# A two-layer hybrid decoder trunk: stacked keys and queries by transfers within SBUF, and latents and conv gates left unscaled ahead of their norms

## The chip, the cores and the metric

The kernel runs on one core of one Trainium2 chip. The metric is device time in microseconds for one execution of the whole program, the median over runs.

## The reference

Two layers over 1024 tokens with a model width of 1024, all in float32. Each layer normalises its input, projects it once, splits the result among four mixers, normalises each mixer's output, projects back, and then runs a gated feed-forward block of width 2816.

```python
def rmsnorm(x, g):
    y = x * lax.rsqrt(jnp.mean(x * x, axis=-1, keepdims=True) + 1e-6)
    return y * g

for l in range(2):
    proj = rmsnorm(x, attn_norm[l]) @ w_in[l]
    (c_q, c_kv, k_r, g_b, g_c, u_conv, u_pool, q_sw, k_sw, v_sw) = jnp.split(proj, pts, axis=-1)
    # 4 heads; q = rmsnorm(c_q) @ w_uq, k, v = rmsnorm(c_kv) @ w_ukv, one shared rotary key k_r
    y_a = mla_attention(c_q, c_kv, k_r, ...)
    y_b = g_b * causal_conv3(g_c * u_conv)
    y_c = multiscale_pool(u_pool, pool_w[l], pool_scale[l])
    # 4 query heads, 2 key heads of 64, window 128, sinks
    y_d = swa_sink_attention(q_sw, k_sw, v_sw, swa_sinks[l], slopes)
    mixed = concat(rms(y_a), rms(y_b), rms(y_c), rms(y_d)) * mix_norm[l]
    x = x + mixed @ w_o[l]
    gate, up = jnp.split(rmsnorm(x, ffn_norm[l]) @ w_gate_up[l], 2, axis=-1)
    x = x + (silu(gate) * up) @ w_down[l]
return rmsnorm(x, final_norm)
```

## The kernel before

Everything is held transposed: 128 channels on the partitions, tokens along the free axis, in two halves t of 512 tokens. A matrix product in float32 is made from three fast products: each operand is split into a high part (a cast to fp32r, by ScalarE, `act`) and a low part (the operand less the high part, by VectorE, `dve`). `split`, `half_split` (L278 to L291) do that, and `mm3` (L269) issues the three matmuls per 128 rows of contraction. A square tile of 128 channels by 512 tokens has a contraction over 8 such blocks, so 24 matmuls.

SBUF is handed out by `Slots` as 47 places of 128 x 1024 values, each a pair of halves; freed places go to the back of a queue. A tile that takes a place over waits until everything that used the place is done. PSUM has eight banks with the tags mm (2), s (3), t (2) and pv (1). All bulk loads and stores are issued by `sp` (SyncE), in the order of its queue; an issue whose wait isn't over holds up those behind it. Weights are fetched one step ahead by `expect`, `take` and `ahead`. The program is written as one sequence, and a scheduler decides, when the kernel is built, the order of the instructions on each engine, so that matmuls of the next projection stand between the short steps of attention. That order is then fixed.

A layer's first part goes so:

- `SumSq` adds up squares of the layer's input; its `rnorm` (L323) sums over the partitions by a matmul with ones (L327) and makes r, the reciprocal root mean square, with Ln, Exp, Square and one correction step (L329 to L335). The projections run on the input without r, and each result is multiplied by r (`mul_to`, L339) when it leaves PSUM.
- Window attention's keys (`kk`, L462 to L471): the projection has key head 0 in rows 0 to 63 (`hd`) and head 1 in rows 64 to 127 (`tl`). Each head is wanted in both halves of a tile, once as high parts, once as low parts. ScalarE copies 64 rows to their own place and to the other half (L468, L469), VectorE makes the low parts for both (L470, L471).
- Window queries (`swa_q`, L417 to L432): for two heads e and o, one tile holds the high part of a head in one half and its low part in the other, so that two matmuls (L502, in `swa_unit`) do for a score block what three would.
- `conv` (L626) makes (u r)(C r), a convolution over three tokens, and multiplies with (B r). The second half of its channels, `conv(1)`, runs later, between the first steps of latent attention.
- Latent queries `cq` and keys `ckv` (from L730) are scaled by r, split with the gain, squared and summed (`sq_q`, `sq_kv`), and their own norm factor is applied later: for queries in the rotary tables `tq`, for keys before the split.
- The rotary key goes by a matmul with a selection matrix (L778) to rows 64 to 127; both key sets `kb_[0]` and `kb_[1]` get it by a split each. `keys(hp)` (L835) projects two heads' keys at a time and splits rows 0 to 63 and 64 to 127 of the result into rows 0 to 63 of `kb_[0]` and `kb_[1]`.
- `scores` (L863; matmuls L887 to L889), `mix_values` (L933), `out_some` and the feed-forward part follow. The steps over (head, half) are in `steps`; `keys(1)` runs at the fifth of them.

Of the kernel before, what the change touches and what calls it, by code (L numbers as in the profile page):

```python
# [13 lines left out]
AF = mybir.ActivationFunctionType  # L14
# [3 lines left out]
P = 128  # L18
# [92 lines left out]
def trunk_kernel(ctx: ExitStack, tc: tile.TileContext, ins, out):  # L111
# [183 lines left out]
    class SumSq:  # L295


        def __init__(self, n):
            self.n = n
            self.acc = [None, None]  # L300
            self.done = {}

        def add(self, t, f, cols=whole):
# [11 lines left out]
            act.activation(q, f, AF.Square)  # L315
            if m == self.n // P:
                dve.scalar_tensor_tensor(
                    out=a, in0=q, scalar=e, in1=a, op0=ALU.add, op1=ALU.add
                )
            else:  # L320
                dve.tensor_tensor(out=a, in0=a, in1=q, op=ALU.add)

        def rnorm(self, t, cols=whole, tag="t"):  # L323

            a, n = F.ap(self.acc[t])[:, cols], self.n
            p = ps(tag)[:, cols]
            pe.matmul(p, ones, a, start=True, stop=True)  # L327
            r0, q = tmp("tn")[:, cols], tmp("tn")[:, cols]
            act.activation(r0, p, AF.Ln, scale=1.0 / n)  # L329
            act.activation(r0, r0, AF.Exp, scale=-0.5)  # L330
            act.activation(q, r0, AF.Square)
            dve.scalar_tensor_tensor(
                out=q, in0=p, scalar=-0.5 / n, in1=q, op0=ALU.mult, op1=ALU.mult
            )
# [8 lines left out]

    hd = slice(0, 64)
    tl = slice(64, 128)

    x_in = ins["xT"]
    ss = SumSq(D)
# [11 lines left out]
    def enter_norm(t):  # L360
        for k in range(NK):
            ss.add(t, F.ap(xf[k][t]))
            F.free(xf[k][t])
        ratt[t] = ss.rnorm(t)

    def finish(x, t, cols):

# [10 lines left out]
    for l in range(L):  # L378
# [38 lines left out]
        def swa_q(m, pp):  # L417
            for t in range(2):
                f = tmp()
                dve.scalar_tensor_tensor(  # L420
                    out=f, in0=pp[t], scalar=0.125, in1=r_of(t), op0=ALU.mult, op1=ALU.mult
                )
                e, o = R.half(), R.half()
                qs[2 * m][t], qs[2 * m + 1][t] = e, o
                act.copy(R.ap(e)[hd], f[hd])
                act.copy(R.ap(o)[tl], f[tl])
                dve.tensor_tensor(
                    out=R.ap(e)[tl], in0=f[hd], in1=rd(R.ap(e)[hd]), op=ALU.subtract
                )
                dve.tensor_tensor(  # L430
                    out=R.ap(o)[hd], in0=f[tl], in1=rd(R.ap(o)[tl]), op=ALU.subtract
                )  # L432

        wk = take()
        if l == 0:
# [24 lines left out]
        pq = [proj(w, 0, "s"), proj(w, 1, "t")]  # L460
        ahead()
        kk = [[R.pair(), R.pair()] for _ in range(2)]  # L462
        for t in range(2):
            f = tmp()
            mul_to(f, pk[t], r_of(t))
            for g, own, oth in ((0, hd, tl), (1, tl, hd)):
                k1, k2 = R.ap(kk[g][0] + t), R.ap(kk[g][1] + t)
                act.copy(k1[own], f[own])  # L468
                act.copy(k1[oth], f[own])  # L469
                dve.tensor_tensor(out=k2[own], in0=f[own], in1=rd(k1[own]), op=ALU.subtract)  # L470
# [130 lines left out]

        def group_scale(g):

            sg = SumSq(2 * P)
# [21 lines left out]
        def conv(ct):  # L626

            z = F.pair()
            pp = project()
            for t in range(2):  # L630
                mul_to(F.ap(z + t), pp[t], r_of(t))
            yield
            pp = project()
            for t in range(2):
                f = tmp()
                mul_to(f, pp[t], r_of(t))
                mul_to(F.ap(z + t), F.ap(z + t), f)
# [21 lines left out]
            yield  # L659

        for _ in conv(0):
            swa_some(3)
        swa_q(1, project())
# [66 lines left out]
        sq_q = SumSq(2 * P)  # L730
# [10 lines left out]
        sq_kv = SumSq(P)  # L741
# [15 lines left out]
        for t in range(2):  # L757
# [424 lines left out]
        pieces = (0, 3, 2, 2, 1, 1, 2, 2)  # L1182
        conv1 = conv(1)
        next(conv1)
        group_scale("d")
        keys(0)
        group_split("d", 1)
# [2 lines left out]
        for n, (h, t) in enumerate(steps):  # L1190
# [8 lines left out]
            if n == 0:  # L1199
                group_split("d", 0)  # L1200
                next(conv1)
                for k in range(NK):
                    for u in range(2):
                        for s in hh[k][u]:
                            R.free(s)
                for u in range(2):
                    F.free(ratt[u])
                qn = queries(*steps[1])
                values()
                group_scale("b")  # L1210
                group_split("b", 1)
                group_split("b", 0)
                fetch_x()
                fetch_x()
# [366 lines left out]
        for n, (c, m) in enumerate(units):  # L1581
# [41 lines left out]
            elif c == B22:  # L1623
                done(2 * m, 1)
                if m == 0:
                    expect_layer(l + 1)
                    ahead()
                if m == 1:
                    ratt[0] = ss.rnorm(0, tag="pv")
                if m == NM - 1:  # L1630
                    ratt[1] = ss.rnorm(1, tag="pv")
# [139 lines left out]
```

## Time and profile before

| | |
|---|---|
| median of 3 runs | 2094.0 us (2093.92 to 2096.62) |
| span of the profiled execution | 2092.6 us |
| TensorE busy (PE) | 2057.8 us, 98% |
| VectorE busy (DVE) | 1493.1 us, 71% |
| ScalarE busy (ACT) | 977.7 us, 47% |
| GpSimd busy (POOL) | 539.8 us, 26% |
| granted TensorE clock, mean | 0.998 |

The span runs from the first to the last instruction of one profiled execution; the runs' times are taken without the profiler, and the median lies 1.4 us above the span. "PEld" is TensorE's loading of weights, which overlaps the matmuls. In a group's row, the columns are line, engine, operation, output from inputs by the program's names, shapes, and the count; behind the first bar the busy time in us and the mean of one in ns; behind the second the idle time of the engine just before, and who ended it. In a row of waits stand the waiting engine, tile and line, the releaser, and then the sum in us, the number and the longest. A stretch's row has the stretch, its length, busy time and count for PE, PE's loads, DVE, ACT and POOL, the granted clock, the DMA engines' busy share and GB/s. A DMA row has the tile, the issuing queue, the count, the size and the median time in us from issue to landing. u stands for any tile of `Slots`, te, tn and tp for short-lived tiles, vraw for a small raw weight.

### The profile page before, as it was taken

What the parts mean: (1) busy time and instruction counts of PE and PEld (TensorE: products, weight loads), DVE (VectorE), ACT (ScalarE), POOL (GpSimd) and SP (SyncE); (2) the same over time, 40 slices, a digit from 0 to 9 for tenths busy, and PEclk for the clock granted to TensorE, in tenths of its full rate; (3) what the DMA queues carried; (4) which work ended last, traced back from release to release, by engine and by line L of the source; (5) the groups of instructions that cost most, each with busy time, mean ns of one, the idle gap of its engine ahead of it and who ended that gap; (6) DMA issues with size and microseconds to landing.
All of it is one profiled execution on the core that took longest, in us unless ns stands there. A gap on an engine that the chain in (4) does not pass through costs nothing.

```text
span 2092.6 us, 26301 instructions
## 1 busy us (share of the span) xinstructions
PE 2057.8 (98%) x9442; PEld 1679.2 (80%) x9442; DVE 1493.1 (71%) x2407; ACT 977.7 (47%) x1706; POOL 539.8 (26%) x453
## 2 busy tenths in 40 slices
PE   8999999999999999999999999999999999999997
PEld 6777787888888888888888777877878888888887
DVE  6878977877666767566656889869666676675655
ACT  6446656653333334454433566657423333344442
POOL 0000000037676674200000000000467667541000
PEclk9999999999999999999999999999999999999999
DMA  4010122424444446886401102232354444378752
GB/s 178 33 51 26 68 87 73 161 72 169 172 156 151 166 161 201 290 289 220 147 28 51 46 13 92 68 117 100 112 180 161 143 174 156 126 259 312 260 178 88
DMA packets 148819, 289.76 MB, mean 138 GB/s; under 512 B 12608, under 2 KB 72000, under 8 KB 148688
## 3 DMA queue, kind: packets, MB, share of 16 engines
q1 hardware_dynamic: 148656, 288.03, 39.8%
q8 instruction: 74, 1.21, 0.2%
q14 instruction: 57, 0.47, 0.1%
q0 software_dynamic: 32, 0.04, 0.0%
HBM read 204.66 MB, written 83.36 MB: 138 GB/s over the span
## 4 chain that ended last, share of the span: by engine, by line
PE 92%; DVE 4%; ACT 2%; DMA 1%; issue 1%; POOL 0%; DVEq 0%; ACTq 0%; SPq 0%; POOLq 0%
PE ps_mm L269 35%; PE ps_s L269 28%; PE ps_t L269 12%; PE ps_pv L269 8%; PE ps_pv L953 2%; PE ps_t L941 1%; PE ps_t L327 1%; PE ps_s L887 1%; PE ps_pv L563 1%; PE ps_s L888 1%; PE ps_t L551 1%; PE ps_s L889 1%; PE ps_s L502 0%; DMA u<-in_w_o 0%; DVE u L281 0%
## 5 line engine op out<-in xcount | busy, mean ns | idle before, releaser
L269 PE MATMUL ps_mm<-u,u 128*128 128x512 f32 (+1 forms) x3376 | 825.2, 391 | 10.6 <-ACT u L283 6.9
L269 PEld LDWEIGHTS ps_mm<-u,u 128*128 128x128 f32 x3376 | 616.8, 189 | 132.9 <-ACT u L283 6.9
L269 PE MATMUL ps_s<-u,u 128*128 128x512 f32 x2672 | 630.8, 390 | 3.5 <-ACT tn L1167 3.5
L269 PEld LDWEIGHTS ps_s<-u,u 128*128 128x128 f32 x2672 | 501.5, 188 | 110.4 <-ACT tn L1167 4.3
L281 DVE TENSOR_TENSOR u<-u,u 128x1024 fp32r<-128x1024 f32 (+2 forms) x368 | 423.6, 1167 | 175.5 <-ACT u L280 155.3
L280 ACT CAST u<-u 128x1024 fp32r<-128x1024 f32 (+2 forms) x368 | 321.4, 897 | 485.1 <-PE ps_mm L269 182.3
L269 PE MATMUL ps_t<-u,u 128*128 128x512 f32 (+1 forms) x1212 | 274.5, 379 | 0.0
L269 PEld LDWEIGHTS ps_t<-u,u 128*128 128x128 f32 x1212 | 219.1, 188 | 44.1 <-issue 1.4
L950 POOL MEMSET u<- 128x128 f32 x32 | 6.4, 225 | 870.5 <-PE ps_mm L269 653.5
L158 POOL TENSOR_TENSOR u<-u 128x256 f32<-128x256 f32 x176 | 187.0, 1063 | 92.6 <-DMA u<-in_w_dn 62.7
L1303 POOL TENSOR_TENSOR tp<-tp,u 128x512 f32<-128x512 f32 x88 | 127.0, 1444 | 291.2 <-ACT tp L1302 290.9
L269 PE MATMUL ps_pv<-u,u 128*128 128x512 f32 x696 | 164.9, 389 | 0.0
L269 PEld LDWEIGHTS ps_pv<-u,u 128*128 128x128 f32 x696 | 130.7, 188 | 27.1
L1302 ACT ACTIVATE tp<-tp 128x512 f32<-128x512 f32 x88 | 55.5, 632 | 123.0 <-DVE tp L339 122.1
L280 ACT CAST u<-ps_t 128x512 fp32r<-128x512 f32 (+4 forms) x136 | 66.3, 505 | 67.4 <-PE ps_t L941 42.8
L281 DVE TENSOR_TENSOR u<-ps_t,u 128x512 fp32r<-128x512 f32 (+4 forms) x136 | 77.5, 582 | 25.7 <-ACT u L280 24.8
L283 ACT ACTIVATE u<-u,par 128x512 fp32r<-128x512 f32 x100 | 69.4, 715 | 51.2 <-DVE u L1090 16.5
L1123 POOL TENSOR_TENSOR u<-u,u 128x512 f32<-128x512 f32 x38 | 65.6, 1727 | 85.5 <-PE ps_s L269 44.5
L284 DVE SCALAR_TENSOR_TENSOR u<-u,par,u 128x512 fp32r<-128x512 f32 x100 | 72.8, 745 | 9.4 <-ACT u L283 9.1
L1515 DVE TENSOR_TENSOR tp<-ps_mm,tn 128x512 f32<-128x512 f32 x38 | 26.3, 692 | 68.7 <-PE ps_mm L269 68.7
L213 DVE TENSOR_TENSOR u<-u,u 128x1024 fp32r<-128x1024 f32 (+1 forms) x46 | 51.7, 1128 | 29.0 <-PE ps_t L269 10.0
L1296 DVE SCALAR_TENSOR_TENSOR u<-te,tp 128x512 f32<-128x512 f32 x38 | 44.9, 1182 | 36.8 <-POOL tp L1303 36.8
(188 smaller groups left out, 2248.7 us busy)
## 6 DMA issues: line engine op xcount, KB each, us to landing
u<-in_w_gu SPq DMA_DIRECT2D x88, 512.0 KB, 4.0
ad<-u SPq DMA_DIRECT2D x154, 256.0 KB, 2.2
u<-ad SPq DMA_DIRECT2D x70, 512.0 KB, 5.4
u<-in_w_dn SPq DMA_DIRECT2D x68, 512.0 KB, 3.8
qd<-u SPq DMA_DIRECT2D x44, 512.0 KB, 2.9
u<-qd SPq DMA_DIRECT2D x32, 512.0 KB, 5.2
u<-in_w_in SPq DMA_DIRECT2D x30, 512.0 KB, 3.5
u<-in_xT SPq DMA_DIRECT2D x32, 256.0 KB, 4.5
```

Source lines behind the costliest of these rows:

```text
L158: pool.tensor_tensor(out=o, in0=o, in1=u, op=ALU.add)
L213: dve.tensor_tensor(out=lo[:, :n], in0=raw[:, :n], in1=rd(hi[:, :n]), op=ALU.subtract)
L269: pe.matmul(o, w, r, start=start and k == 0 and i == 0, stop=stop and k == n - 1 and i == 2, skip_group_check=again,)
L280: act.copy(hi, f)
L281: dve.tensor_tensor(out=lo, in0=f, in1=rd(hi), op=ALU.subtract)
L283: act.activation(hi, f, AF.Copy, scale=gain)
L284: dve.scalar_tensor_tensor(out=lo, in0=f, scalar=gain, in1=rd(hi), op0=ALU.mult, op1=ALU.subtract)
L953: pe.matmul(py[:, c0:], v_of(j, h), R.ap(s)[:, c0:], start=j == 0 and n == 0, stop=j == nj - 1 and n == 1,)
L1123: pool.tensor_tensor(out=F.ap(q + 1), in0=a21, in1=a22, op=ALU.add)
L1296: dve.scalar_tensor_tensor(out=o, in0=a, scalar=-1.0, in1=b, op0=ALU.mult, op1=ALU.mult)
L1302: last_silu = act.activation(g, g, AF.Silu)
L1303: pool.tensor_tensor(out=g, in0=g, in1=r, op=ALU.mult)
```

## The change

1. `move(o, a)` is an SBUF to SBUF transfer issued by SyncE. It takes the place of casts and subtractions that made the same values a second time in another half of the partitions: for the window keys (six transfers of 64 rows by 1024 columns a layer, two of them after the other four have read), the window queries (two for each of four tiles, the second after the first, for it writes what the first reads), the rotary key and the latent keys (two for each half of the tokens, and four for each half and head pair; 64 rows by 512).
2. Latent queries and keys are no longer multiplied by r. Their norm is taken of the raw projection, with eps divided by r squared: c r / sqrt(mean((c r)^2) + eps) = c / sqrt(mean(c^2) + eps / r^2). `rnorm` with `more` keeps eps / r^2 (as eps times the mean square of the input, from the same PSUM bank) and r^2, and `SumSq` with `eps` adds the first in. The query latents are read in PSUM by cast, subtraction and square.
3. In `conv`, u is multiplied by r^2, C is used as it is and so is B; group b's norm gets eps / r^2.
4. r is freed after the second product of `conv(1)`, the eps tiles after group b's norm.

```diff
@@ SumSq.add
             if m == 1:
                 act.activation(a, f, AF.Square)
-                if self.n == P:
+                if self.eps:
+                    dve.scalar_tensor_tensor(
+                        out=a, in0=F.ap(self.eps[t]), scalar=float(self.n // P),
+                        in1=a, op0=ALU.mult, op1=ALU.add,
+                    )
+                elif self.n == P:
                     dve.tensor_scalar(out=a, in0=a, scalar1=e, scalar2=None, op0=ALU.add)
                 return
...
-            if m == self.n // P:
+            if m == self.n // P and not self.eps:
@@ SumSq.rnorm
             act.activation(r0, p, AF.Ln, scale=1.0 / n)
             act.activation(r0, r0, AF.Exp, scale=-0.5)
+            if more:
+                self.more[t] = F.half(), F.half()
+                r2, e = (F.ap(i) for i in self.more[t])
+                act.activation(e, p, AF.Copy, scale=EPS / n)
...
+            if more:
+                act.activation(r2, a, AF.Square)
@@
+    def move(o, a):
+        sp.dma_start(rd(o), rd(a))
@@ swa_q
-                e, o = R.half(), R.half()
+                e, o, h = R.half(), R.half(), R.half()
                 qs[2 * m][t], qs[2 * m + 1][t] = e, o
+                split(R.ap(h), R.ap(o), f)
                 act.copy(R.ap(e)[hd], f[hd])
-                act.copy(R.ap(o)[tl], f[tl])
-                dve.tensor_tensor(
-                    out=R.ap(e)[tl], in0=f[hd], in1=rd(R.ap(e)[hd]), op=ALU.subtract
-                )
-                dve.tensor_tensor(
-                    out=R.ap(o)[hd], in0=f[tl], in1=rd(R.ap(o)[tl]), op=ALU.subtract
-                )
+                move(R.ap(e)[tl], R.ap(o)[hd])
+                move(R.ap(o)[hd], R.ap(h)[tl])
+                R.free(h)
@@ window keys
+        f = F.pair()
         for t in range(2):
-            f = tmp()
-            mul_to(f, pk[t], r_of(t))
-            for g, own, oth in ((0, hd, tl), (1, tl, hd)):
-                k1, k2 = R.ap(kk[g][0] + t), R.ap(kk[g][1] + t)
-                act.copy(k1[own], f[own])
-                act.copy(k1[oth], f[own])
-                dve.tensor_tensor(out=k2[own], in0=f[own], in1=rd(k1[own]), op=ALU.subtract)
-                dve.tensor_tensor(out=k2[oth], in0=f[own], in1=rd(k1[own]), op=ALU.subtract)
+            mul_to(F.ap(f + t), pk[t], r_of(t))
+        split(*(R.ap2(i) for i in kk[0]), F.ap2(f))
+        F.free_pair(f)
+        for a, b in zip(kk[0], kk[1]):
+            for rows in (hd, tl):
+                move(R.ap2(b)[rows], R.ap2(a)[tl])
+        for a in kk[0]:
+            move(R.ap2(a)[tl], R.ap2(a)[hd])
@@ conv
-                mul_to(F.ap(z + t), pp[t], r_of(t))
+                mul_to(F.ap(z + t), pp[t], F.ap(rr[t][0]))
...
-                f = tmp()
-                mul_to(f, pp[t], r_of(t))
-                mul_to(F.ap(z + t), F.ap(z + t), f)
+                mul_to(F.ap(z + t), pp[t], F.ap(z + t))
...
-                f = tmp()
-                mul_to(f, pp[t], r_of(t))
-                mul_to(F.ap(ac + t), F.ap(ac + t), f)
+                mul_to(F.ap(ac + t), pp[t], F.ap(ac + t))
@@ latent queries and keys
-                f = tmp()
-                mul_to(f, pp[t], r_of(t))
-                cq[m][t] = half_split(f, pcol(l, PC_QN + m))
-                sq_q.add(t, f)
+                cq[m][t] = half_split(pp[t], pcol(l, PC_QN + m))
+                sq_q.add(t, pp[t])
...
-            mul_to(F.ap(s), pp[t], r_of(t))
+            act.copy(F.ap(s), pp[t])
@@ rotary key
             for s in range(2):
                 kb_[s][0][t], kb_[s][1][t] = R.half(), R.half()
-                split(R.ap(kb_[s][0][t])[tl], R.ap(kb_[s][1][t])[tl], p[tl])
+            split(R.ap(kb_[0][0][t])[tl], R.ap(kb_[0][1][t])[tl], p[tl])
+            for n in range(2):
+                move(R.ap(kb_[1][n][t])[tl], R.ap(kb_[0][n][t])[tl])
@@ keys
-                for s, own in ((0, hd), (1, tl)):
-                    split(R.ap(kb_[s][0][t])[hd], R.ap(kb_[s][1][t])[hd], p[own])
+                hl = half_split(p)
+                for n in range(2):
+                    for s, own in ((0, hd), (1, tl)):
+                        move(R.ap(kb_[s][n][t])[hd], R.ap(hl[n])[own])
+                    R.free(hl[n])
```

More of the change, by code (lines that the diff above doesn't have):

```diff
@@ L295, in trunk_kernel, with __init__ @@
     class SumSq:
-        def __init__(self, n):
+        def __init__(self, n, eps=None):
             self.n = n
+            self.eps = eps
             self.acc = [None, None]
             self.done = {}
+            self.more = [None, None]
         def add(self, t, f, cols=whole):
@@ L310, in add @@
                 act.activation(a, f, AF.Square)
-                if self.n == P:
+                if self.eps:
+                    dve.scalar_tensor_tensor(
+                        out=a,
+                        in0=F.ap(self.eps[t]),
+                        scalar=float(self.n // P),
+                        in1=a,
+                        op0=ALU.mult,
+                        op1=ALU.add,
+                    )
+                elif self.n == P:
                     dve.tensor_scalar(out=a, in0=a, scalar1=e, scalar2=None, op0=ALU.add)
@@ L321, in add, with rnorm @@
                 dve.tensor_tensor(out=a, in0=a, in1=q, op=ALU.add)
-        def rnorm(self, t, cols=whole, tag="t"):
+        def rnorm(self, t, cols=whole, tag="t", more=False):
             a, n = F.ap(self.acc[t])[:, cols], self.n
@@ L363, in enter_norm @@
             F.free(xf[k][t])
-        ratt[t] = ss.rnorm(t)
+        ratt[t] = ss.rnorm(t, more=True)
     def finish(x, t, cols):
@@ L602, in group_scale @@
         def group_scale(g):
-            sg = SumSq(2 * P)
+            sg = SumSq(2 * P, rr_eps if g == "b" else None)
             for t in range(2):
@@ L654, in conv @@
             for t in range(2):
-                f = tmp()
-                mul_to(f, pp[t], r_of(t))
-                mul_to(F.ap(ac + t), F.ap(ac + t), f)
+                mul_to(F.ap(ac + t), pp[t], F.ap(ac + t))
             y["b"][ct] = [ac, ac + 1]
             yield
+        rr = ss.more
+        rr_eps = [e for _, e in rr]
         for _ in conv(0):
@@ L729, in trunk_kernel @@
         cq = [[None, None], [None, None]]
-        sq_q = SumSq(2 * P)
+        sq_q = SumSq(2 * P, rr_eps)
         for m in range(2):
@@ L740, in trunk_kernel @@
         ckv = [None, None]
-        sq_kv = SumSq(P)
+        sq_kv = SumSq(P, rr_eps)
         pp = project()
@@ L1184, in trunk_kernel @@
         next(conv1)
+        for u in range(2):
+            F.free(ratt[u])
+            F.free(rr[u][0])
         group_scale("d")
@@ L1205, in trunk_kernel @@
                             R.free(s)
-                for u in range(2):
-                    F.free(ratt[u])
                 qn = queries(*steps[1])
@@ L1210, in trunk_kernel @@
                 group_scale("b")
+                for i in rr_eps:
+                    F.free(i)
                 group_split("b", 1)
@@ L1628, in trunk_kernel @@
                 if m == 1:
-                    ratt[0] = ss.rnorm(0, tag="pv")
+                    ratt[0] = ss.rnorm(0, tag="pv", more=not last)
                 if m == NM - 1:
-                    ratt[1] = ss.rnorm(1, tag="pv")
+                    ratt[1] = ss.rnorm(1, tag="pv", more=not last)
         for cols in (slice(0, 256), slice(256, HT)) if last else ():
```

## The prediction

> **What bounds the kernel now.** I read the page's head first, then the chain in order of time, the stretches of the span, and last TensorE's own waits.
>
> ```profile
> span 2092.6 us, 26301 instructions
> PE 2057.8 (98%) x9442; PEld 1679.2 (80%) x9442; DVE 1493.1 (71%) x2407; ACT 977.7 (47%) x1706; POOL 539.8 (26%) x453
> L269 PE MATMUL ps_mm<-u,u 128*128 128x512 f32 (+1 forms) x3376 | 825.2, 391 | 10.6 <-ACT u L283 6.9
> ...
> 404.28 5.44 PE ps_mm L269 x24
> ```
>
> TensorE is the bound: the span is its matmuls end to end. 24 of them in a row take 5.44 us, 0.227 us each, though one record lasts 0.391: they overlap, so each idle stretch shown below costs about 0.16 us more than it shows. The change adds and removes no matmul, so it can only move the idle places. Where they lie (the mixers run in the first five stretches of layer 0 and in 1077 to 1440 of layer 1):
>
> ```profile
> 8.00:60.00 52.00, 49.74 (x211) 39.58 (x212) 41.63 (x65) 35.55 (x60) 0.00 (x0) 1.00 0.38 144
> 60.00:205.00 145.00, 144.06 (x687) 113.43 (x686) 117.14 (x284) 78.48 (x185) 0.00 (x0) 1.00 0.12 40
> 205.00:260.00 55.00, 53.04 (x249) 42.17 (x248) 53.23 (x115) 36.13 (x78) 0.34 (x2) 1.00 0.18 63
> 260.00:345.00 85.00, 84.61 (x438) 67.99 (x436) 69.73 (x194) 52.80 (x134) 2.05 (x10) 1.00 0.24 76
> 345.00:405.00 60.00, 58.29 (x264) 45.98 (x265) 45.87 (x73) 34.22 (x58) 0.76 (x4) 1.00 0.42 147
> 405.00:1077.00 672.00, 670.64 (x2950) 553.43 (x2949) 443.69 (x501) 275.66 (x376) 268.20 (x208) 1.00 0.51 175
> 1077.00:1235.00 158.00, 157.26 (x752) 124.35 (x750) 121.63 (x292) 80.90 (x190) 0.00 (x0) 1.00 0.11 37
> 1235.00:1290.00 55.00, 53.07 (x248) 42.19 (x247) 53.26 (x113) 36.36 (x80) 0.35 (x2) 1.00 0.18 58
> ```
>
> The columns are the stretch, its length, then busy time of PE, PE's loads, DVE, ACT, POOL. Length less PE is idle: 2.26, 0.94, 1.96, 0.39, 1.71 in layer 0; 0.74 and 1.93 in layer 1 to 1290. In 205 to 260 and its twin DVE is busy 53.23 of 55, so it is the late engine there; elsewhere it has room. The idle of the stretches that hold the edited projections (first three, and the two of layer 1) is 2.26+0.94+1.96+0.74+1.93 = 7.8 us: about all that can be won.
>
> ```profile
> PE ps_t L327 <- DVE u L317: 2.2, 4, 0.9
> PE ps_s L887 <- ACT u L280: 2.0, 2, 1.0
> PE ps_mm L269 <- ACT u L212: 1.7, 2, 1.1
> PE ps_mm L269 <- ACT tn L315: 0.9, 1, 0.9
> PE ps_s L502 <- DVE u L430: 0.5, 1, 0.5
> ...
> 231.27 0.69 DVE L339 TENSOR_TENSOR te<-ps_s,u 128x512 f32<-128x512 f32 x1
> 232.00 0.62 ACT L280 CAST u<-te 128x512 fp32r<-128x512 f32 x1
> 232.67 0.50 PE L887 MATMUL ps_s<-u,u 128*128 128x512 f32 x1 [1.04 <-ACT u L280]
> ```
>
> The largest in 205 to 260 is read as a chain: the first latent query is scaled by DVE at 231.27, cast by ACT at 232.00, and the first score matmul starts at 232.67 after 1.04 idle. DVE came to that scaling late, behind the second conv half's products.
>
> **The change part by part.** Prices:
>
> ```profile
> L339 DVE TENSOR_TENSOR te<-ps_mm,u 128x512 f32<-128x512 f32 x22 | 15.1, 684 | 1.3 <-PE ps_mm L269 1.1
> L281 DVE TENSOR_TENSOR u<-ps_s,u 64x512 fp32r<-64x512 f32 x8 | 5.5, 685 | 0.8 <-ACT u L280 0.6
> L213 DVE TENSOR_TENSOR u<-u,u 128x1024 fp32r<-128x1024 f32 x15 | 18.1, 1219 | 5.4 <-PE ps_mm L269 4.4 <-PE ps_pv L563 1.0
> L332 DVE SCALAR_TENSOR_TENSOR tn<-ps_t,tn 128x512 f32<-128x512 f32 x14 | 9.6, 688 | 9.8 <-ACT tn L331 9.6
> L483 DVE TENSOR_TENSOR u<-ps_t,u 128x256 fp32r<-128x256 f32 x4 | 1.7, 418 | 0.3 <-ACT u L482 0.3
> L283 ACT ACTIVATE u<-u,par 128x512 fp32r<-128x512 f32 x45 | 30.8, 713 | 11.4 <-DVE u L339 5.1 <-DVE u L1090 5.1 <-DMA par<-in_params 0.7
> L212 ACT CAST u<-u 128x1024 fp32r<-128x1024 f32 x15 | 15.7, 1049 | 13.2 <-DMA u<-in_w_in 12.2 <-DVE u L580 0.7 <-DVE tn L332 0.3
> L330 ACT ACTIVATE tn<-tn 128x512 f32<-128x512 f32 x14 | 8.9, 633 | 0.3
> L280 ACT CAST u<-ps_s 64x512 fp32r<-64x512 f32 x8 | 4.7, 582 | 3.0 <-PE ps_s L269 2.9
> L482 ACT CAST u<-ps_t 128x256 fp32r<-128x256 f32 x4 | 1.5, 364 | 1.1 <-DVE u L483 1.1
> L941 PE MATMUL ps_t<-cst,u 128*128 128x128 f32 x144 | 23.3, 273 | 0.7 <-DVE u L281 0.7
> ...
> vraw<-in_w_uq SPq DMA_DIRECT2D x16, 128.0 KB, 2.1
> ad<-u SPq DMA_DIRECT2D x154, 256.0 KB, 2.2
> vraw<-in_pool_w SPq DMA_DIRECT2D x2, 128.0 KB, 5.1
> u<-ad SPq DMA_DIRECT2D x14, 256.0 KB, 5.9
> ...
> L209 SPq DMA_DIRECT2D vraw<-in_w_uq x16: 327/328/770, 27.6 to 1312.7; - x16
> ...
> L470 DVE TENSOR_TENSOR u<-te,u x8: 677/687/689, 40.4 to 1065.4; 64x512 fp32r<-64x512 f32 x8
> L427 DVE TENSOR_TENSOR u<-te,u x8: 684/685/686, 57.0 to 1138.1; 64x512 fp32r<-64x512 f32 x8
> ```
>
> A 64-row operation costs what a 128-row one does (0.685 against 0.684), so copying halves by engine is dear. Per layer DVE loses: window keys, eight subtractions for one of 1024 columns (8x0.687-1.219 = 4.3 us); one subtraction for each of four query tiles (2.7); two for the rotary key, four for the latent keys (4.1); four conv products (2.7, and as many for the second conv half, 2.7); four query-latent scalings, two key-latent ones which go to ACT (4.1). It gains two multiply-adds for the query latents and two for conv's group norm (2.8). Net about 18 us a layer. ACT loses some 7 us (seven casts of the window keys, six of 64 rows) and gains some 4 (four eps copies and squares of r, two copies of the key latent, 0.6 each). Nearly all of this lies under matmuls and is worth nothing by itself; with the cover gone it would be its length.
>
> *Gain in 205 to 260.* In the 26 us ahead of 231.27 fall four conv products and two key subtractions fewer and one or two multiply-adds more: 6x0.685-2x0.688 = 2.7 us of a DVE that never rests there. The query's scaling needs to come 1.04+0.16 earlier: all of that stall goes. The other stall (L327 behind L317, 0.9) is the group norm of the conv channels, whose chain gets one operation of 0.69 longer while its queue gets 2.7 shorter: I take half, 0.45. Bounds 0 and 1.96; taken 1.5 a layer, 3.0 in all.
>
> *Gain in 8 to 60.* DVE is rid of eight subtractions, ACT of seven casts, around the norm chain. Waits there that these feed: 0.9 and 0.5, with 0.16 each on top. Bounds 0 and 1.7; taken 0.8, since the two new ACT operations (1.2) stand in the norm's own queue.
>
> *Cost: the window keys wait for two transfers in a row.* In the changed order the first window score stands behind 74 matmuls of 512 columns and 8 transposes after the second norm's sum (50 and 8 before): 74x0.227+8x0.11 = 17.7 us of cover (a transpose is a record of 0.273 less the same 0.16). The chain, by rows: four ACT operations (0.6, 0.6, 0.63, 0.63) and a weight cast 1.05 = 3.5; three on DVE = 5.6; the 1024 cast and subtraction = 7.8. SP issues in order, and the second transfer of the first query stands behind the first of the second query, whose source DVE makes eight operations later (0.42+0.69+0.68+0.42+0.68+1.22+0.42+0.69 = 5.2): 13.0; one issue slot of 0.33 and a landing of 2.2: 15.5. It fits by 2.2, so nothing. With landings of 5.9 the two in a row decide: the first query is split at 7.8+0.42+0.69 = 8.9, two landings and an issue later it is 21.0, 3.3 late. In layer 1 the keys are done near 1065 and the first queries near 1138: 70 us of room.
>
> *Cost: the latent keys of the second head pair.* Between the last of their first-half matmuls and the first score that reads them stand 10 matmuls and 8 transposes: 3.1 us. Chain: tail 0.16, cast 0.58, issue and landing 2.1: 2.8, and 3.2 with an issue slot of 0.33; the low half has 1.8 us more and needs one subtraction more. Bounds 0 and (landing 5.1) 3.1 a layer; no row shows a transfer between partitions of SBUF, and the nearest is the unhurried 128 KB load, 2.1. Taken 0.3 a layer, 0.6. Behind these eight issues on SP stand an output weight piece and the next query weights, tens of matmuls from use: nothing. The first head pair has 20 us of cover.
>
> [...]
>
> *Cost: raw latents stay in PSUM.* A query-latent bank was free after one product (0.68). Now a cast, a multiply-subtract and ACT's square read it, and in ACT's order the first half's square stands behind the second half's cast, a copy, a pool evacuation and another cast: 0.16+0.71+0.36+0.71+0.63+0.63 = 3.2 after the second half's matmuls, against 2.3 us of other matmuls before the bank's next use; for the next product, without the evacuation and one cast, 1.9 against 1.4. Bounds 0 and 1.4 a layer; taken 0.6, 1.2 in all, since that order was laid with such waits in view.
>
> *Nothing:* four more half tiles of norm factors held through the end of layer 0, and an earlier release of r: TensorE idles 1.36 in all of 405 to 1077, and what is loaded there has room. If one load came late by it, its landing, 2.2 to 5.9.
>
> *Sum:* -3.0-0.8+0.6+1.2 = -2.0. The span is 2092.6 and the median of the runs 2094.0, 1.4 above it; what lies around the span stays. Forecast 2092.0.
>
> **Rivals.** *The relief reaches further.* DVE at 18 us less a layer also shortens the chains between scores and transposes, and all idle of the edited stretches goes: 2094.0-7.8 = 2086.2. For it: DVE is a releaser in most waits above. Against: 1.7 of it is weights arriving, and window scores keep their own latency.
>
> *Transfers land late (slower).* If landings are those of the busy rows (5.1 to 5.9) rather than the quiet ones, the place is the second head pair in both layers, 3.1-0.3 = 2.8 more each, and the start of layer 0, 3.3: 8.9 over the forecast, 2100.9. It begins at a landing of 2.1 and passes 0.2% near 5. For: SP's issues are in order and each transfer waits for its source. Against: the DMA share in the stretches of these transfers is 0.11 to 0.38, and the load of 5.9 belongs to the stretch at 0.50 and the one of 5.1 happens once a layer.
>
> *It does nothing:* engines are relieved where matmuls cover them and the order of matmuls shifts the stalls rather than ending them: 2094.
>
> **How the numbers follow.** Forecast 0.42, its own range 2088 to 2097; further relief 0.28; late transfers 0.23; nothing 0.07. Range 2084 to 2102: it reaches to both rivals. 0.2% is 4.2 us, about what a measurement tells from no change: faster (under 2089.8) takes 0.26 of the relief case and 0.09 of the forecast's, 0.35; slower (over 2098.2) 0.20 of the late transfers and 0.03, 0.23; the rest, 0.42, is the same.
>
> **What would show it.** Right: DVE busy down by some 35 us; the 1.04 before the first latent score gone in both layers; 64-row transfers landing in 2 to 2.5 us; no wait of the window scores on a transfer. Wrong: a wait of latent scores (the fifth step) on a transfer over 1 us, or of a projection on the square's release over 1 us a layer; or new idle in 345 to 405 (1.71 now), where another order of tiles in SBUF could move the output weights by some us either way.

## The result, and the profile after

The changed kernel takes 2110.3 us (median of 4 runs, 2108.46 to 2111.69) against 2095.3 for the kernel before on the same chip: a ratio of 1.0068, 95% interval 1.0056 to 1.0081. That is 15 us slower, outside the predicted range.

The page of the profiled execution of the changed kernel: the head, TensorE's first group, and the two DMA rows of the new transfers (the last number is the median landing in us).

```profile
span 2109.7 us, 26415 instructions
...
PE 2066.7 (98%) x9442; PEld 1682.6 (80%) x9442; DVE 1460.9 (69%) x2353; ACT 966.6 (46%) x1692; POOL 536.5 (25%) x453
...
L269 PE MATMUL ps_mm<-u,u 128*128 128x512 f32 (+1 forms) x3376 | 831.0, 392 | 14.8 <-ACT u L283 7.1
...
u<-u SPq DMA_DIRECT2D x56, 128.0 KB, 2.3
...
u<-u SPq DMA_DIRECT2D x12, 256.0 KB, 3.9
```

The count of matmuls is the same, VectorE is 32.2 us lighter, and the idle time in front of the ps_mm group rose from 10.6 to 14.8. The stretches of the changed kernel, in the columns of the prediction (length, busy time of PE, its loads, DVE, ACT, POOL, granted clock, DMA share, GB/s):

```profile
8.00:60.00 52.00, 51.14 (x214) 40.94 (x215) 38.39 (x58) 33.59 (x57) 0.00 (x0) 1.00 0.52 173
60.00:205.00 145.00, 140.41 (x656) 108.82 (x655) 107.84 (x270) 76.37 (x182) 0.00 (x0) 0.98 0.18 51
205.00:260.00 55.00, 54.53 (x252) 42.89 (x250) 46.49 (x99) 32.42 (x70) 0.34 (x2) 1.00 0.23 68
...
345.00:405.00 60.00, 57.27 (x270) 45.23 (x270) 46.05 (x83) 33.20 (x60) 0.76 (x4) 1.00 0.41 145
405.00:1077.00 672.00, 670.38 (x2949) 553.10 (x2948) 441.52 (x503) 277.52 (x381) 264.81 (x208) 1.00 0.52 178
1077.00:1235.00 158.00, 152.78 (x723) 120.19 (x723) 108.69 (x272) 74.60 (x180) 0.00 (x0) 0.99 0.16 48
1235.00:1290.00 55.00, 54.53 (x244) 42.50 (x243) 44.26 (x88) 31.63 (x65) 0.35 (x2) 1.00 0.25 70
```

Length less PE: the idle of 8 to 60 fell from 2.26 to 0.86, that of 205 to 260 from 1.96 to 0.47 and of its twin from 1.93 to 0.47, which are the predicted gains. But 60 to 205 went from 0.94 to 4.59 and 1077 to 1235 from 0.74 to 5.22, and in both the granted clock is below 1. TensorE's own timeline shows the place in layer 0 (start, length, instruction, in brackets the idle time before it and who ended it):

```profile
162.85 1.43 PE L269 MATMUL ps_mm<-u,u 128*128 128x512 f32 x5 [1.08 <-ACT tn L326]
...
189.64 0.51 PE L269 MATMUL ps_s<-u,vhi 128*128 128x512 f32 x1 [1.55 <-ACT u L283]
...
190.75 0.66 PE L269 MATMUL ps_s<-u,vhi 128*128 128x512 f32 x1 [0.16 <-DVE u L284]
...
192.33 2.42 PE L269 MATMUL ps_mm<-u,u 128*128 128x512 f32 x4 [0.50 <-ACT u L212]
```

At 189.64 the latent keys of the first head pair wait for the key latent's split (L283); at 192.33 the first projection of conv(1) waits for the cast of its weights (L212). Its first four matmuls then take 2.42 us, where four at 0.227 are 0.9: the clock. Stretches of 3.41 us, cut where the clock changes, in the changed kernel:

```profile
187.49:190.90 3.41, 1.70 (x5) 0.69 (x6) 3.41 (x7) 1.62 (x3) 0.00 (x0) 1.00 0.00 0
190.90:194.31 3.41, 2.91 (x6) 1.40 (x7) 3.25 (x6) 2.69 (x4) 0.00 (x0) 0.50 0.34 77
194.31:197.73 3.42, 3.42 (x8) 2.00 (x7) 1.72 (x2) 0.39 (x1) 0.00 (x0) 0.50 0.02 5
...
1228.63:1232.04 3.41, 2.13 (x6) 0.97 (x6) 3.32 (x7) 1.85 (x4) 0.00 (x0) 0.99 0.13 29
1232.04:1235.45 3.41, 3.11 (x7) 1.82 (x6) 3.18 (x4) 1.34 (x2) 0.00 (x0) 0.51 0.22 50
...
1549.41:1552.82 3.41, 0.80 (x4) 0.67 (x5) 2.91 (x3) 2.54 (x4) 2.20 (x2) 1.00 0.13 45
1552.82:1556.23 3.41, 3.41 (x10) 2.63 (x9) 0.41 (x1) 0.00 (x0) 3.33 (x3) 0.50 0.53 149
```

Four stretches ran at half clock, those at 190.90, 194.31, 1232.04 and 1552.82. TensorE was busy in 12.85 us of them, and half of that, 6.4 us, is by estimate what the clock cost: the matmuls at 194.54 and 194.97 start 0.43 us apart, those at 197.87 and 198.10, at full clock again, 0.23. The kernel before had no such stretch until its last 9 us. With the idle time of all stretches, which is 8.1 us larger than before (the two bad stretches 8.1, the three good ones -4.35, the rest of both layers 4.4), that makes 14.5 of the 17.1 us between the two spans; part of the rest is the 0.16 that every further stall hides in its record, by the prediction's estimate. The clock's part is not one of this execution alone: the mean granted clock was 0.994 or 0.995 in all four executions of the changed kernel, and 0.998 on average in those of the kernel before. One less the granted clock, times the span, gives 11.6 us against 4.7, the last microseconds at half clock included in both.

Why conv(1)'s weights came late is told by ScalarE. Its timeline, first of the changed kernel, then of the kernel before:

```profile
188.87 0.72 ACT L283 ACTIVATE u<-u,par 128x512 fp32r<-128x512 f32 x1 [0.57 <-DVE u L356]
190.63 0.58 ACT L280 CAST u<-ps_t 64x512 fp32r<-64x512 f32 x1 [1.04 <-PE ps_t L792]
191.23 1.04 ACT L212 CAST u<-u 128x1024 fp32r<-128x1024 f32 x1
```

```profile
164.68 1.05 ACT L212 CAST u<-u 128x1024 fp32r<-128x1024 f32 x1 [0.77 <-DMA u<-in_w_in]
```

The load was issued at 150.65 in the changed kernel and landed 3.6 us later, long before 191. What held the cast is the place that it writes. ScalarE's instruction order in the built programs, with the position, the places (u and a number) and the engines or DMA queues (DMAHW) whose semaphores each waits for, first the changed kernel, in the last line the kernel before:

```
171 L759 TensorCopy u24_1676<-ps_mm_1620 128x512 [waits DVE_49,PE_49]
196 L283 Activation u32_1690<-u24_1676,par_75 128x512 [waits DVE_49]
198 L212 TensorCopy u24_1773<-u44_1771 128x1024 [waits DMAHW5_49,DVE_49]
...
165 L212 TensorCopy u12_1782<-u27_1780 128x1024 [waits DMAHW0_49,PE_49]
```

Place 24 holds the raw key latent (written by L759, split by L283); the high part of conv(1)'s weights gets the same place and must wait for the split. Places are handed out in turn, the longest free first. r squared and the eps terms hold two of them, so 7 are free when this place is handed out instead of 9, and the turn comes to a place given back too recently. With the weights late, the scheduler put the latent keys ahead: counted in TensorE's own work (0.227 us for each 512-column matmul), they stand at 165 us instead of 177, with conv(1)'s 48 matmuls behind them rather than in front. The chain to the keys then has 48 matmuls, 10.9 us, less to hide under.

### The profile page after: what moved, and what is told of

Its sections match the earlier page's. It is cut to its first block, busy times and chain, and to the rows that moved or that the text cites. A ratio compares the mean times of both kernels' runs of the same rounds, so it can differ in the third digit from the quotient of the medians.

```text
span 2109.7 us, 26415 instructions
## 1 busy us (share of the span) xinstructions
PE 2066.7 (98%) x9442; PEld 1682.6 (80%) x9442; DVE 1460.9 (69%) x2353; ACT 966.6 (46%) x1692; POOL 536.5 (25%) x453
## 4 chain that ended last, share of the span: by engine, by line
PE 88%; DVE 4%; ACT 3%; DMA 2%; issue 1%; POOL 1%; DVEq 0%; SPq 0%; ACTq 0%; POOLq 0%
PE ps_mm L269 34%; PE ps_s L269 27%; PE ps_t L269 11%; PE ps_pv L269 7%; PE ps_pv L972 2%; PE ps_t L960 1%; PE ps_t L338 1%; PE ps_pv L581 1%; PE ps_t L569 1%; PE ps_s L906 1%; ACT u L280 1%; DVE u L281 1%; PE ps_s L907 1%; PE ps_s L908 1%; DMA u<-in_w_o 1%
## 5 line engine op out<-in xcount | busy, mean ns | idle before, releaser
L269 PE MATMUL ps_mm<-u,u 128*128 128x512 f32 (+1 forms) x3376 | 831.0, 392 | 14.8 <-ACT u L283 7.1
L158 POOL TENSOR_TENSOR u<-u 128x256 f32<-128x256 f32 x176 | 182.3, 1036 | 94.8 <-DMA u<-in_w_dn 61.7
L281 DVE TENSOR_TENSOR u<-ps_t,u 128x512 fp32r<-128x512 f32 (+3 forms) x132 | 75.0, 580 | 31.0 <-ACT u L280 30.5
L283 ACT ACTIVATE u<-u,par 128x512 fp32r<-128x512 f32 x100 | 70.1, 716 | 51.2 <-DVE u L1109 19.0
L280 ACT CAST u<-ps_t 128x512 fp32r<-128x512 f32 (+3 forms) x132 | 64.0, 503 | 54.4 <-PE ps_t L960 31.9
L326 ACT ACTIVATE tn<-u 128x512 f32<-128x512 f32 (+1 forms) x93 | 53.4, 589 | 36.0 <-DVE u L1590 30.9
```

The source lines that it names most:

```text
L158: pool.tensor_tensor(out=o, in0=o, in1=u, op=ALU.add)
L269: pe.matmul(o, w, r, start=start and k == 0 and i == 0, stop=stop and k == n - 1 and i == 2, skip_group_check=again,)
L280: act.copy(hi, f)
L281: dve.tensor_tensor(out=lo, in0=f, in1=rd(hi), op=ALU.subtract)
L283: act.activation(hi, f, AF.Copy, scale=gain)
```

## The experiments

Theory A is what was just said: places, hence order, hence stalls, hence clock. Rival B: the raw latents made the chain to the keys longer, and it would be late in any order. Rival C: the transfers, and what stands behind them on SyncE, cost it. Ratios are against the kernel before on the same chip, with 95% intervals.

**e1, e2: each half of the change alone.** e1 undoes `SumSq`'s eps, `more`, and the edits in `conv`, `cq` and `ckv`; e2 undoes the four edits with `move`.

> The transfers of the change alone; latents, conv gates and norms as in the kernel before. In the instruction order the second conv half's first 48 matmuls stand ahead of the latent keys, as before. Theory A (the loss comes from the raw latents' two more places held, which put the second conv half's weights into the key latent's place, so that the latent keys come 12 us earlier on TensorE and wait there): no loss, 2089 to 2096. Rival C (the transfers cost it): 2104 to 2111.

> Raw latents, raw conv gates and eps over the square of r alone; stacking by engine operations as before, no transfers. The latent keys stand ahead of the second conv half, as in the changed kernel. Theory A and rival B (the key latent's norm chain itself got later): the loss is here, 2104 to 2113, with the granted clock falling once a layer. Rival C: 2088 to 2096.

e1: 2097.6 us, 1.0004 (0.9995 to 1.0013). e2: 2115.0, 1.0087 (1.0072 to 1.0102). Each lies some 2 us above its range, but the two are 17 us apart, and rival C is out: the half with the transfers comes out even, and all of the loss is in the other. Even is a sum, though: e1 wins 1.5 us of idle in 8 to 60 and loses 1.1, and a stretch at half clock, in 345 to 405. The stretch of 160 to 205, first e1, then e2:

```profile
160.00:205.00 45.00, 43.94 (x187) 32.20 (x186) 36.78 (x71) 30.68 (x60) 0.00 (x0) 1.00 0.15 42
```

```profile
160.00:205.00 45.00, 41.40 (x165) 28.53 (x164) 35.27 (x67) 32.43 (x61) 0.00 (x0) 0.92 0.03 12
```

e2 has 3.6 us of idle there and a clock of 0.92; the kernel before has 0.20 and 1.00, and e1 1.06 and 1.00.

**e3, e4: one place more**, in the changed kernel and in the kernel before.

```diff
-N_U = 47
+N_U = 48
-    pool.dma_start(par, ins["params"])
+    act.dma_start(par, ins["params"])
-    nc = _bacc.Bacc("TRN2", target_bir_lowering=False, num_devices=1, dynamic_dma_scratch_size=2048)
+    nc = _bacc.Bacc("TRN2", target_bir_lowering=False, num_devices=1, dynamic_dma_scratch_size=64)
```

> The changed kernel with one place more in SBUF (48; the room comes from the scratch of GpSimd's DMA queue, and the parameters are loaded by ScalarE's queue). The cast of the second conv half's weights moves in ScalarE's order from 59 instructions behind the rotary key's weights to 4 behind; half of its matmuls come ahead of the first rotary selection, the latent keys stay at the same depth of TensorE's work (165.9 us against 165.2). Theory A: a good part of the stall of 187 to 198 goes with the clock drop, 2097 to 2104. Rival B: 2107 to 2111.

> The kernel before with the same one place more. With it the latent keys move in TensorE's order from 177 us of work to 165, ahead of the second conv half, as in the changed kernel, though nothing else is edited. Theory A in the form that the order of TensorE is what costs: 2100 to 2108, a stall at the latent keys and a clock drop. Rival B (the chain got longer by the edit): no loss without the edit, 2092 to 2096.

Both missed every expectation: 2151.4 (1.0260) and 2150.7 (1.0260). The further place changed the order in the feed-forward part as well, where TensorE now waits some 22 and 18 us, for 3.5 before, for the copy of a bank by ScalarE (`snap`); so the times say nothing of the theory. One stretch of e4 does. Its timeline at the latent keys, and two stretches of 3.41 us (the profiled execution took 2140.5):

```profile
188.16 0.50 PE L269 MATMUL ps_s<-u,vhi 128*128 128x512 f32 x1 [1.49 <-ACT u L283]
...
192.65 0.50 PE L269 MATMUL ps_s<-u,vhi 128*128 128x512 f32 x1 [1.67 <-ACT u L283]
```

```profile
185.40:188.81 3.41, 1.78 (x7) 0.92 (x5) 3.41 (x7) 2.05 (x3) 0.00 (x0) 1.00 0.61 221
188.81:192.22 3.41, 1.88 (x6) 1.05 (x6) 3.38 (x6) 2.73 (x5) 0.00 (x0) 1.00 0.56 221
```

The kernel before, not edited but for a place, shows the same stall at the same line once its latent keys come early (165 us of work). No raw latent is needed for it, against B. The clock stayed at 1.00, though TensorE idled 1.63 and 1.53 of the two stretches.

**e5, e6, e7: the changed kernel with the order or the place put right.** e5 moves the first latent keys behind conv(1)'s 48 matmuls by the PSUM tag; e6 gives conv(1)'s weights, once a layer, the places that the ring of weights has just given back; e7 does both.

```diff
@@ keys (e5, e7)
-            p = ps("s")
+            p = ps("s" if hp else "mm")
@@ ring_next (e6, e7; lifo is set around the ahead() between the rotary key's halves)
             ring_drop()
+            if lifo[0]:
+                slots.places.rotate(2)
```

> The changed kernel; the first head pair's latent keys take their PSUM banks from tag mm, whose two banks the second conv half's first products hold, so that they stand behind these 48 matmuls on TensorE (179.5 us of work instead of 165.2). The cast of that half's weights still waits for the key latent's place. Theory A in two parts (the place makes the cast late, the order puts the keys first): the wait moves from the keys to the cast, little gain, 2104 to 2110. If the keys' position alone costs: 2097 to 2102. Rival B (the raw latents' longer norm chain is late by itself): 2107 to 2111.

> The changed kernel; the second conv half's weights take the places that the ring of weights has just given back instead of the oldest free ones. Their cast waits for TensorE's key latent product, not for the key latent's split. 24 of that half's 48 matmuls come ahead of the latent keys (170.9 us of work). Theory A: half or more of the stall and the clock drop go in both layers, 2098 to 2105. Rival B: the keys and the rotary selection wait as before, 2107 to 2111.

> The changed kernel with both edits: weights in the places given back, latent keys of the first head pair behind all 48 matmuls (179.0 us of work). That is nearly the order of the kernel before, with the raw latents, the eps chain and the transfers of the change. Theory A: the stalls of 187 to 198 and their clock drops go, 2096 to 2101; what is left over the kernel before are the projections that wait for the square of raw latents, some 2 a layer. Rival B: 2106 to 2111.

e5: 2111.7, 1.0076 (1.0059 to 1.0093). e6: 2101.5, 1.0029 (1.0018 to 1.0039). e7: 2103.1, 1.0034 (1.0022 to 1.0046). Two rotated places, with nothing else in the source touched, take back 8.8 of the 15 us. Moving the keys alone takes back nothing: e5 lies just above the ranges of both theories, which overlap, so its time doesn't part them; but in its timeline the wait goes to the rotary key and to the cast of the weights.

```profile
189.66 0.49 PE L792 MATMUL ps_t<-u,e_r 128*128 128x512 f32 x1 [1.77 <-DVE u L281]
191.89 0.80 PE L269 MATMUL ps_mm<-u,u 128*128 128x512 f32 x2 [1.74 <-ACT u L212]
```

In e6 the cast comes at 176.74 and the stalls at the keys and at conv(1)'s first products are gone. But layer 0 idles as much as in the changed kernel (3.47 us in 160 to 205, for 3.44): another stall has taken their place, before a norm's sum. First e6's stretch, then the stall:

```profile
160.00:205.00 45.00, 41.53 (x170) 30.13 (x171) 35.40 (x67) 30.32 (x58) 0.00 (x0) 0.96 0.18 48
```

```profile
200.00 1.90 PE L341 MATMUL ps_t<-u,ones 128*128 128x512 f32 x2 [2.35 <-DVE u L284]
```

What came back is three of the four stretches at half clock, and idle in layer 1 (1190 to 1240: 2.19 for 4.07). So the place is the cause of the late cast and of the keys' early position; that it is the cause of the time, e6 shows for a part, and e13 below for most. e7 missed its numbers by 2 us and isn't told apart from e6. It idles less at 160 to 205 (2.34 against 3.47), but loses two stretches at half clock near 1540, where e6 loses none.

**e8: latents scaled again, on top of e7** (`cq`, `ckv`, `sq_q` and `sq_kv` as before; raw gates and transfers stay).

> As the run before, and query and key latents scaled by r when they leave PSUM as in the kernel before, their norms without eps over the square of r; conv gates stay raw and the transfers stay. Theory A with the undersized cost of latents held in PSUM: the waits for the square go too, 2091 to 2096. If the latents held in PSUM cost nothing: as the run before, within 2.

2099.6, 1.0017 (1.0008 to 1.0027): 3.5 less than e7, missed by 4. The waits for the square of a raw latent are gone as expected. Two stretches at half clock (near 1350 and 1540) remain, as many as e7 has.

**e9, e10, e11: parts that should keep the gains.** e9 is the kernel before with the window keys and queries by transfers; e10 adds raw gates with e6's places; e11 is raw gates with e6's places and no transfer.

> The kernel before; window keys and window queries stacked by transfers, everything else as before (rotary and latent keys by engine operations, latents and gates scaled). The instruction order at the latent keys is that of before. Theory: the first 60 us gain some 1.5 and nothing else changes, 2093 to 2096. Rival (each edit shuffles the places and with them stalls elsewhere, the gain is lost again): 2096 to 2100.

> As the run before, and conv gates raw with r squared and the eps term, the second conv half's weights in the places given back; latents scaled. Theory: the gains of 8 to 60 and of 205 to 260 (1.4 a layer) both stand, the loss at the latent keys is some 2 a layer, 2091 to 2096. Rival: the latent keys, 6 us earlier on TensorE than before, still wait and drop the clock, 2097 to 2102.

> Conv gates raw with the second conv half's weights in the places given back; no transfers, latents scaled. Theory: the gain of 205 to 260 in both layers (2.8) against some 2 a layer at the latent keys, 2092 to 2098. Rival: as in the run before, 2098 to 2103.

e9: 2093.7, 0.9992 (0.9983 to 1.0001). e10: 2097.8, 1.0011 (1.0002 to 1.0019). e11: 2103.2, 1.0039 (1.0027 to 1.0052). e9 came as expected. e10 and e11 missed their ranges and came out at the rival's times (e11 just above), but not by its mechanism: the latent keys do not stall (idle at 160 to 205: 1.36 and 1.38, clock 1.00). What e11 lost lies elsewhere, above all here:

```profile
345.00:405.00 60.00, 55.95 (x248) 43.45 (x248) 42.55 (x69) 30.78 (x52) 0.76 (x4) 0.97 0.40 138
```

4.05 of idle and a clock drop, at stalls that the kernel before has too (1.71 in all). Why they grow there was not tried apart.

**e12, e13: raw gates, and then the whole change, without any place held.** u r is multiplied by r once more by GpSimd, which in the kernel before is busy 0.00 us of 8 to 205 and of 1077 to 1235, in place of a stored r squared; the two eps halves get tiles of their own (the room comes from the same two lines as in e3). e12 has window transfers and scaled latents, e13 is the whole change.

```diff
+    epst = [cpool.tile([P, HT], F32, name=f"eps{t}") for t in range(2)]
@@ rnorm
-                self.more[t] = F.half(), F.half()
-                r2, e = (F.ap(i) for i in self.more[t])
-                act.activation(e, p, AF.Copy, scale=EPS / n)
+                act.activation(epst[t], p, AF.Copy, scale=EPS / n)
...
-            if more:
-                act.activation(r2, a, AF.Square)
@@ conv
-                mul_to(F.ap(z + t), pp[t], F.ap(rr[t][0]))
+                mul_to(F.ap(z + t), pp[t], r_of(t))
+                pool.tensor_tensor(out=F.ap(z + t), in0=F.ap(z + t), in1=r_of(t), op=ALU.mult)
```

> Window keys and queries by transfers, conv gates raw, latents scaled, latent and rotary keys by engines; but no place of the 47 is held for it: u times r is multiplied by r again by GpSimd, which is idle there, in place of a stored r squared, and the two eps halves have tiles of their own (room from the scratch of GpSimd's DMA queue; the parameters are loaded by ScalarE's queue). The instruction order at the second conv half and the latent keys is then that of before (keys at 177.2 us of work). Theory A: no loss at 160 to 205 and its twin, the gains of 8 to 60 (1.5) and part of 205 to 260 stand, 2089 to 2094. Rival (the raw gates cost by their own chain, not by the places): 2096 to 2101.

> The whole change, raw latents and all transfers included, with the places relieved as in the run before. The weights of the second conv half are cast early and half of its matmuls stand ahead of the latent keys (170.9 us of work; before 177.2, the changed kernel 165.2). If places and order are all: 2096 to 2101, as the run with the early places. If the raw latents cost much by themselves: 2103 to 2110.

e12: 2091.6, 0.9982 (0.9973 to 0.9991). e13: 2097.5, 1.0008 (0.9999 to 1.0018). Both as theory A had it. Without the held places the whole change costs nothing that can be told from no change, where it cost 15 us; the norm chain is rid of ScalarE's squares of r as well, which was not tried apart. e13's profiled execution took 2103.1, above the median, and even there the bad stretch has lost most of its idle and its clock drop, with the raw latents in place:

```profile
160.00:205.00 45.00, 43.61 (x183) 31.56 (x182) 38.24 (x71) 32.68 (x63) 2.21 (x2) 1.00 0.18 48
```

Its twin, 1190 to 1240, idles 1.35 instead of 4.07. Over all its executions the clock takes 4.8 us, as in the kernel before (4.7); by the same count e6 loses 6.8 and the changed kernel 11.6. e12 beats both kernels, by 3.9 us against the one before. The stretches of e12:

```profile
8.00:60.00 52.00, 51.51 (x217) 41.34 (x218) 37.51 (x57) 32.02 (x54) 2.91 (x2) 1.00 0.52 168
...
160.00:205.00 45.00, 44.33 (x189) 32.79 (x188) 37.87 (x72) 32.65 (x63) 2.60 (x2) 1.00 0.08 24
205.00:260.00 55.00, 53.76 (x257) 42.85 (x255) 53.56 (x119) 35.81 (x78) 0.35 (x2) 1.00 0.20 61
```

Idle of 8 to 60: 0.49 against 2.26 before; of 205 to 260: 1.24 against 1.96, and 1.19 against 1.93 in the twin: 3.2 us. The rest is not of the edit's making as far as is known: the waits for `snap` in the feed-forward part are 2.5 instead of 3.5, 160 to 205 idles 0.67 instead of 0.20, and one stretch at 347 runs at half clock, as in e1, e11 and e13 but not in the kernel before.

## Why the prediction was wrong, point by point

**The bound: right.** No matmul came or went, and the idle places and the clock account for nearly all of the difference. VectorE fell by 32 us for a predicted 35, and that was worth nothing by itself.

**Gain in 205 to 260: right**, 1.5 in each layer, as predicted. It comes from the raw half: with transfers alone (e1) the stretch idles 1.98 as before. Not at the same places, though: the 1.04 before the first latent score is gone in e1 too, and 1.15 stands at 219.18 instead, where a product waits for the cast of its weights (L212).

**Gain in 8 to 60: right in kind, too small**: 1.4 for 0.8. e1 has it too (0.77 left), and so has e9 (0.63), so it is the window stacking's. A third wait there, 0.36 at L478, went with the 0.9 and the 0.5 that were counted.

**Transfers: right.** No wait of TensorE on one stands among the waits of the changed kernel, and e1 is even. The landings were 2.3 us at 128 KB, for a predicted 2.1 to 2.2. At 256 KB a 64-row transfer took 3.9, outside the 2 to 2.5 that was named, and the 128-row store of the same size (ad from u) 2.2; but the six of a layer are issued one behind the other (in layer 0 the DMA engines are busy 0.87 of 51 to 62), so what is due to the rows isn't shown. The rival built on late transfers fell with this: slower it was, by another mechanism.

**Raw latents in PSUM: right in kind, half the size.** Predicted 0.6 a layer; the projection waits 1.08 for the square in each layer, 1.24 with the hidden 0.16. The square's chain was followed correctly and the midpoint taken because the order "was laid with such waits in view", which is no reason.

**"Nothing: four more half tiles ... TensorE idles 1.36 in all of 405 to 1077, and what is loaded there has room": the step that failed.** It looked for the price of held places where they are held longest, and took it for a late landing of 2.2 to 5.9. The stretch of 405 to 1077 indeed lost only 0.26. The price fell where a chain hung on the place that came next in turn: a cast 26 us later (191 for 165), since its destination was a tile of another chain, and from it another order on TensorE. With e6's two rotated places 8.8 us came back, with no place held (e13) 12.8. That the latent keys stand 12 us earlier in TensorE's order could be read from the order of both kernels before any run. The prediction read that order for the window scores, the second head pair and the query latents' banks; of the first head pair it asked only what lies behind its keys ("20 us of cover"), and not what had gone from in front of them.

**What it had no term for: the clock**, 6.4 us. The third drop shows that a stall's cost depends on where it falls. TensorE's timeline at the start of the feed-forward part of layer 1, in the kernel before, the changed kernel, e2 and e6:

```profile
1536.26 3.01 PE L269 MATMUL ps_s<-u,u 128*128 128x512 f32 x12 [2.10 <-ACT tn L1167]
```

```profile
1552.02 4.60 PE L269 MATMUL ps_s<-u,u 128*128 128x512 f32 x12 [2.85 <-ACT tn L1186]
```

```profile
1557.88 3.03 PE L269 MATMUL ps_s<-u,u 128*128 128x512 f32 x12 [2.88 <-ACT tn L1183]
```

```profile
1542.85 3.06 PE L272 MATMUL ps_s<-u,u 128*128 128x512 f32 x12 [2.80 <-ACT tn L1191]
```

The changed kernel idles 0.75 more than the kernel before, and the 12 matmuls behind take 1.6 us longer. e2 and e6 idle as long as it does, and their 12 matmuls take no longer than before: the stall falls otherwise on the clock's grid (last section). These 1.6 us are bad luck of the grid, and that e6 is without them is good luck, not the two places.

**A rival's argument that was misread**: "1.7 of it is weights arriving", against all 7.8 us of idle being won. Those waits (L212, 1.1 and 0.6) lie in 345 to 405 and its twin, and are no part of the 7.8.

**Named as signs of a wrong prediction**: the projection's wait for the square over 1 us a layer, and new idle in 345 to 405 (2.73 for 1.71, behind the sums of a group norm). Both came. The larger loss was at neither.

**Still open**: what of the 6 to 7 us that e6 and e7 keep over the kernel before is not the 1.24 a layer of the squares. Some of it is the stall before a norm's sum near 200 (2.35 in e6, 1.97 in e7, 0.78 in e8, where latents are scaled); why it is not in e13, which has the raw latents, was not tried. e13 wins 4 us back with no place held; the rest are short stalls and single clock drops that move with every edit.

## What to carry to other kernels

Where tiles share places that are handed out in turn, a tile held longer changes which place every later tile gets: compare the instruction order of the bound engine in both kernels at each chain it touches, and cost a late cast or load by the work that no longer covers it. A factor kept in scarce space can be cheaper recomputed by an idle engine or kept in a tile outside the turn (e12 and e13 do both at once; e13 takes 12.8 us less than the changed kernel). Add up short stalls over a few microseconds: here 1.55 and 0.16 us of idle in one stretch of 3.41 were followed by a granted clock of 0.50, and 1.63 in one and 1.53 in the next, in e4, were not.

## What the hardware showed unexpectedly

The clock's drops come on a fixed grid in these profiles. In the changed kernel they begin at 190.90, 1232.04 and 1552.82; in its trace each of the last two lasts 3.413 us, the first twice that, and the differences between the starts are 305.0 and 94.0 times 3.413 us. Cut on that grid, the fifteen profiles show up to 2080 us what goes before a drop. All 19 stretches at full clock with 2.0 us or more of recorded idle are followed by one at half clock; of those with less than 1.6, only one is (the 1.28 at 1228.63, made of several short stalls, each with its hidden 0.16); between the two it goes both ways. A stretch already at half clock is followed by another when it idled 0.60 or more, and by none when it idled 0.43 or less. So in these profiles 2.0 us of recorded idle in a stretch of 3.413, in pieces or whole, dropped the clock every time, 0.60 was enough to keep it down, and the phase matters: e4's 3.2 us of idle fell into two stretches and cost no clock, the changed kernel's 1.71 fell into one, with 0.5 behind it, and cost two stretches.
